# Two weight sums of a seven-product block formed by accumulating DMAs, and three plain blocks per call instead of four

## The chip, the cores and the metric

The kernel runs on one core of one Trainium2 chip. The metric is the device time of one execution in microseconds. Three runs of the kernel before the change took 2412.43, 2413.51 and 2416.30 us; the median is 2413.51 us.

## The reference

The program is two layers of an encoder trunk on 512 tokens of 1024 channels. Each layer has a feed-forward part, a mixer, a cross attention to 256 memory tokens, and a second feed-forward part, so the feed-forward part is called four times. The change touches nothing but this part:

```
def rms_norm(x, g):
    xf = x.astype(jnp.float32)
    y = xf * lax.rsqrt(jnp.mean(xf * xf, axis=-1, keepdims=True) + RMS_EPS)
    return (y * g.astype(jnp.float32)).astype(x.dtype)

def swiglu(x, w_in, w_out):
    gate, up = jnp.split(x @ w_in, 2, axis=-1)
    return (jax.nn.silu(gate) * up) @ w_out

# per layer
x = x + 0.5 * swiglu(rms_norm(x, norm_ffn1[l]), ffn1_wi[l], ffn1_wo[l])
...
x = x + 0.5 * swiglu(rms_norm(x, norm_ffn2[l]), ffn2_wi[l], ffn2_wo[l])
```

The hidden width is 2816, which is 22 blocks of 128.

## The kernel before

Everything is kept with channels on the 128 partitions and the 512 tokens along the free side. A float32 matmul is replaced by three matmuls of float32r operands: every operand is split into a high part, made by a copy on ScalarE (`act`, line 76), and a low part, the rest, made by VectorE (`tt`, line 70, or `stt`, line 73). TensorE then adds high x high, high x low and low x high (`mm3`, line 156; all of its matmuls carry line 79). Weights are split on the chip too, right after they are loaded.

A feed-forward call goes through its 22 hidden blocks f = 0 to 21 in order. For a **plain** block it loads the gate and the up weights of the block (512 KB each, into the tag "raw" with two buffers), splits them, and forms both projections with 2 x 24 matmuls of 512 columns (names `pg`, `pu`). Then it applies the norm's factor, SiLU and the product, and splits the result into `fhi` and `flo`.

For a **seven-product** block ("seven") it takes the gate and up rows of the block as a 2 x 2 matrix of quarters: gate and up, each over the first and the second half of the 1024 input channels. The tokens are halved too, 256 and 256. A Strassen-Winograd scheme then needs seven products of 256 columns instead of eight, that is 7 x 4 x 3 = 84 matmuls of 256 columns. It needs four sums of weight quarters (names `ws` in the profile; s1 to s4 in the code), split parts of seven weight operands (`shi`, `slo`, seven buffers each), and sums of the normed input over channel and token halves (`thi`, `tlo`). The input sums are made once per call by `token_sums`, half of them after plain block 1 and half after plain block 2. Products 1, 2 and 3 use the normed input itself (`hhi`, `hlo`), and products 6, 7, 5 and 4 use the sums (`thi`, `tlo`). The products are issued in the order 1, 2, 6, 3, 7, 5, 4, and VectorE joins their results in `z`, `v` and `u`.

The output projection (`second`, names `wr` for its weights and `po` for its products) is done in parts: the hidden blocks are grouped as 0 to 3, 4 to 9, 10 to 15 and 16 to 21 (`PARTS`), and the output products of one group are mixed into the sevens of the next group, a step at a time (`WO_RATE`). While blocks 0 to 3 run, no output products are pending.

What sets the order: the program is written in the order above, and a scheduler turns it into one in-order list for each engine. Instructions of different blocks get interleaved in these lists. Intermediate tiles of this part (`z`, `u`, `v`, the weight sums, the temporaries of the token sums and of the output products) share the tag "t" with eight buffers. Loads are issued by SP's queue, in order; each waits there until the buffer it writes is free. POOL only adds squares at the end of a call.

Of the kernel before, what the change touches and what calls it, by code (L numbers as in the profile page):

```python
# [8 lines left out]
F32 = mybir.dt.float32  # L9
F32R = mybir.dt.float32r  # L10
AF = mybir.ActivationFunctionType
# [4 lines left out]
T = 512  # L16
# [14 lines left out]
REL_MAX = 256  # L31
LEAD, DENSE_RATE, ATT_RATE = 15, (1.0, 0.61, 0.98), 0.65
TURN_RATE = (0.5, 0.9)
PARTS, PLAIN, WO_RATE, WO_LEAD = (0, 4, 10, 16, 22), 4, 0.85, 2

PAR = {}
_n = 0
# [17 lines left out]
def trunk(tc, I, out, depth=DEPTH):  # L55
    nc = tc.nc
    ctx = ExitStack()
    with ctx:
# [8 lines left out]
        mult, add, sub = ALU.mult, ALU.add, ALU.subtract  # L67

        def tt(o, a, b, op, eng=None):
            (eng or nc.vector).tensor_tensor(out=o, in0=a, in1=b, op=op)  # L70

        def stt(o, a, s, b, op0, op1):
            nc.vector.scalar_tensor_tensor(out=o, in0=a, scalar=s, in1=b, op0=op0, op1=op1)

        def act(o, i, f, **k):
            nc.scalar.activation(out=o, in_=i, func=f, **k)  # L76
# [4 lines left out]
        def t2(name, shape=None, dt=F32):  # L81
            return tp.tile(shape or [P, T], dt, tag="t", name=name, bufs=8)
# [7 lines left out]
        def bank(tag, name):  # L90
            return psp.tile([P, T], F32, tag=tag, name=name, bufs=1 if tag in ("po", "ch") else 2)
# [22 lines left out]
        def load_raw(ap, n, step=1024):  # L114
            raw = wp.tile([P, 1024], F32, tag="raw", name="raw", bufs=2)
            for c in range(0, n, step):
                nc.sync.dma_start(out=raw[:, c:min(c + step, n)], in_=ap[:, c:min(c + step, n)])
            return raw
# [9 lines left out]
        def pc(l, n, j=0):  # L128
            o, w = PAR[n]
            return par[:, l, o + j:o + j + 1]  # L130
# [10 lines left out]
        def split(o_hi, o_lo, src):  # L141
            act(o_hi, src, AF.Copy)
            tt(o_lo, src, o_hi.bitcast(F32), sub)
# [12 lines left out]
        def mm3(p, w, v, first, last):  # L156
            (wh, wl), (vh, vl) = w, v
            mm(p, wh, vh, first, False)
            mm(p, wh, vl, False, False)
            mm(p, wl, vh, False, last)  # L160
# [104 lines left out]
        Q = T // 2  # L265

        def ffn(l, which):
            h = norm(l, f"norm_{which}")
            wi, wo = I[f"{which}_wi"][l], I[f"{which}_wo"][l]
            with tc.tile_pool(name="hid", bufs=1) as hidp:  # L270
# [3 lines left out]
                def out(z, u):  # L274

                    hi = hidp.tile([P, T], F32R, tag="fhi", name="fhi", bufs=11)
                    lo = hidp.tile([P, T], F32R, tag="flo", name="flo", bufs=11)
                    split(hi, lo, u)
                    hid.append((hi, lo))
# [22 lines left out]
                def token_sums(ks):  # L302
                    for k in ks:
                        ga, gb = pc(l, f"norm_{which}", k), pc(l, f"norm_{which}", k + 4)
                        xa, xb = x[k], x[k + 4]
                        b1 = t2("b1")
                        act(b1, xa, AF.Copy, scale=ga)
                        s1, s2 = t2("s12"), t2("s34")
                        stt(s1[:, :Q], xa[:, Q:], ga, b1[:, :Q], mult, sub)
                        stt(s1[:, Q:], xb[:, Q:], gb, s1[:, :Q], mult, sub)  # L310
                        stt(s2[:, :Q], xb[:, Q:], gb, b1[:, Q:], mult, sub)
                        stt(s2[:, Q:], xb[:, :Q], gb, s1[:, Q:], mult, sub)
                        for s in (s1, s2):
                            hi = hidp.tile([P, T], F32R, name=f"thi{len(sums)}")
                            lo = hidp.tile([P, T], F32R, name=f"tlo{len(sums)}")
                            split(hi, lo, s)
                            sums.append((hi, lo))
                    if 3 in ks:
                        hidp.tile([P, 72], F32, name="gap")

                def quarter(n):

                    at = {1: (0, 0), 2: (4, 0), 3: (4, 1)}
                    if n in at:
                        k0, c = at[n]
                        t = h[k0:k0 + 4]
                    else:
                        i, c = {5: (0, 0), 6: (0, 1), 7: (1, 0), 4: (1, 1)}[n]
                        t = sums[i::2]
                    return [(hi[:, c * Q:c * Q + Q], lo[:, c * Q:c * Q + Q]) for hi, lo in t]  # L330

                def seven(f):

                    ra, rb = [load_raw(wi[2 * f + i].rearrange("p k m -> p (k m)"), 1024) for i in range(2)]
                    a11, a12, a21, a22 = ra[:, :T], ra[:, T:], rb[:, :T], rb[:, T:]

                    def parts(src):
                        hi = hidp.tile([P, T], F32R, tag="shi", name="shi", bufs=7)
                        lo = hidp.tile([P, T], F32R, tag="slo", name="slo", bufs=7)
                        split(hi, lo, src)  # L340
                        return hi, lo

                    def sums_of(a, b, op):
                        s = t2("ws")
                        tt(s, a, b, op)
                        return s

                    def product(n, p, c, w):

                        for k, v in enumerate(quarter(n)):  # L350
                            s = slice(k * P, k * P + P)
                            mm3(p[:, c * Q:c * Q + Q], (w[0][:, s], w[1][:, s]), v, not c and k == 0, (c or n == 1) and k == 3)

                    def twice(t, c):
                        return t[:, c * Q:c * Q + Q].unsqueeze(1).to_broadcast([P, 2, Q])

                    two = lambda t: t.rearrange("p (c t) -> p c t", c=2)

                    w1 = parts(a11)
                    w2 = parts(a12)  # L360
                    s1 = sums_of(a21, a22, add)
                    s2 = sums_of(s1, a11, sub)
                    w6 = parts(s2)
                    s4 = sums_of(a12, s2, sub)
                    w3 = parts(s4)
                    s3 = sums_of(a11, a21, sub)
                    w7 = parts(s3)
                    w5 = parts(s1)
                    w4 = parts(a22)
                    pa = bank("acc", "p1")  # L370
                    product(1, pa, 0, w1)
                    p1 = t2("p1")
                    act(p1[:, :Q], pa[:, :Q], AF.Copy)
                    yield
                    pb = bank("iv", "p26")
                    product(2, pb, 0, w2)
                    yield
                    product(6, pb, 1, w6)
                    z = t2("z")
                    tt(two(z), two(pb), twice(p1, 0), add)  # L380
                    yield
                    pb = bank("acc", "p37")
                    product(3, pb, 0, w3)
                    yield
                    product(7, pb, 1, w7)
                    v = t2("v")
                    tt(two(v), two(pb), twice(z, 1), add)
                    yield
                    pb = bank("sm", "p54")
                    product(5, pb, 0, w5)  # L390
                    yield
                    product(4, pb, 1, w4)
                    tt(z[:, Q:], pb[:, :Q], v[:, :Q], add)
                    tt(z, z, r, mult)
                    act(z, z, AF.Silu)
                    u = t2("u")

                    tt(two(u)[:, ::-1], two(pb), twice(v, 1), add)
                    tt(u, u, z, mult)
                    out(z, u)  # L400
                    yield

# [26 lines left out]
                for f0, f1 in zip(PARTS, PARTS[1:]):  # L429
                    for f in range(f0, f1):  # L430
                        if f < PLAIN:
                            plain(f)
                            token_sums({1: (0, 1), 2: (2, 3)}.get(f, ()))
                            continue
                        for _ in seven(f):
                            credit += WO_RATE
                            while credit >= 1:
                                credit -= 1
                                next(wos, None)
                    for _ in wos:  # L440
                        pass
                    wos, credit = second(f0, f1, f1 == KF, ("po", "ch") if f1 < KF else ROT[4:] + ROT[:4]), -WO_LEAD
# [785 lines left out]
```

## Time and profile before

| | |
|---|---|
| median of three runs | 2413.51 us |
| profiled execution | 2414.83 us, span 2413.0 us |
| TensorE (PE) busy | 2370.8 us, 98% of the span |
| VectorE (DVE) busy | 1871.7 us, 78% |
| ScalarE (ACT) busy | 1147.8 us, 48% |
| GpSimd (POOL) busy | 177.2 us, 7% |
| bytes moved by DMA | 225.80 MB, mean 94 GB/s |

Busy times come from one execution on the chip. Instructions on VectorE and ScalarE overlap a little at their ends, so the distance from one start to the next is shorter than the duration shown: a two-input VectorE operation of 128 x 512 elements lasts 0.68 us and the next starts 0.60 us later. The ends of matmuls are modelled. In the chain of waits the profile goes back from the last instruction to what released it, step by step; time that stands there is time that set the end. "Issue to landing" is the time from a DMA's issue until its data is there.

### The profile page before, as it was taken

The numbers are of one execution on the slowest core, as the hardware profiler recorded it, in microseconds if no ns is written. First come the engines' busy times: TensorE is split into PE (matmuls) and PEld (weight loads), VectorE is DVE, ScalarE is ACT, GpSimd is POOL, SyncE is SP. The second block draws the span as 40 slices with busy tenths as digits, with TensorE's granted clock in tenths as the row PEclk, the third lists the DMA queues.
The fourth block names the chain that finished last, engine by engine and source line by source line (L and its number), as shares of the span: only waits on it lengthen the run. The fifth ranks groups of instructions, "written<-read, shape, count | busy, mean of one in ns | idle before, by whom it ended". The sixth has DMA issues, their size and how long they took to land.

```text
span 2413.0 us, 43484 instructions
## 1 busy us (share of the span) xinstructions
PE 2370.8 (98%) x17154; PEld 2046.6 (85%) x17154; DVE 1871.7 (78%) x3423; ACT 1147.8 (48%) x2210; POOL 177.2 (7%) x230
## 2 busy tenths in 40 slices
PE   8999999999999999999999999999999999999999
PEld 6999987787789889999889999767877898899997
DVE  7898876767675669988779988757676756699986
ACT  6444444444565554444454444444445655544443
POOL 1000012011110000000100000120111100000001
PEclk9999999999999999999999999999999999999999
DMA  4323332210342222333332333321103422223332
GB/s 155 106 90 107 103 101 100 70 50 26 92 136 93 94 96 92 112 95 101 96 103 94 97 103 105 110 75 62 50 26 92 138 91 94 97 92 112 96 105 83
DMA packets 90973, 225.80 MB, mean 94 GB/s; under 512 B 10224, under 2 KB 27536, under 8 KB 90768
## 3 DMA queue, kind: packets, MB, share of 16 engines
q1 hardware_dynamic: 90768, 223.01, 28.9%
q8 instruction: 135, 2.21, 0.4%
q14 instruction: 70, 0.57, 0.1%
HBM read 215.89 MB, written 7.08 MB: 92 GB/s over the span
## 4 chain that ended last, share of the span: by engine, by line
PE 90%; DVE 5%; issue 2%; ACT 2%; DMA 1%; POOL 0%; POOLq 0%; ACTq 0%; DVEq 0%; SPq 0%
PE p L79 30%; PE po L79 19%; PE pxq L79 5%; PE pin L79 5%; PE pu L79 3%; PE pxw L79 3%; PE pqk L79 3%; PE pg L79 3%; PE pout L79 3%; PE pbvf L79 1%; PE pf L79 1%; PE ptt L79 1%; DVE wlo L70 1%; PE psc L79 1%; PE pxv L79 1%
## 5 line engine op out<-in xcount | busy, mean ns | idle before, releaser
L70 DVE TENSOR_TENSOR wlo<-raw,whi 128x512 fp32r<-128x512 f32 (+3 forms) x326 | 229.7, 712 | 126.9 <-ACT whi L76 119.3
L79 PE MATMUL p<-thi,shi 128*128 128x256 f32 x1152 | 324.9, 282 | 1.5 <-ACT shi L76 1.4
L79 PE MATMUL p<-tlo,shi 128*128 128x256 f32 x1152 | 323.1, 281 | 0.0
L79 PE MATMUL p<-thi,slo 128*128 128x256 f32 x1152 | 322.9, 282 | 0.0
L76 ACT ACTIVATE whi<-raw 128x512 fp32r<-128x512 f32 (+3 forms) x326 | 194.8, 604 | 249.6 <-PE pin L79 47.0
L79 PE MATMUL po<-flo,whi 128*128 128x512 f32 x704 | 277.4, 394 | 0.0
L79 PE MATMUL po<-fhi,wlo 128*128 128x512 f32 x704 | 277.0, 393 | 0.1
L79 PE MATMUL po<-fhi,whi 128*128 128x512 f32 x704 | 276.5, 394 | 0.0
L79 PE MATMUL p<-hlo,shi 128*128 128x256 f32 x864 | 242.9, 281 | 0.0
L79 PE MATMUL p<-hhi,slo 128*128 128x256 f32 x864 | 242.8, 281 | 0.0
L79 PE MATMUL p<-hhi,shi 128*128 128x256 f32 x864 | 242.7, 281 | 0.0
L79 PEld LDWEIGHTS p<-thi,shi 128*128 128x128 f32 x1152 | 216.8, 188 | 17.9 <-ACT shi L76 10.1
L76 ACT ACTIVATE shi<-ws 128x512 fp32r<-128x512 f32 x288 | 173.8, 629 | 104.1 <-DVE ws L70 102.2
L79 PEld LDWEIGHTS p<-tlo,shi 128*128 128x128 f32 x1152 | 217.0, 188 | 7.2
L79 PEld LDWEIGHTS p<-thi,slo 128*128 128x128 f32 x1152 | 216.1, 188 | 4.0 <-DVE slo L70 1.5
L70 POOL TENSOR_TENSOR ssa<-ssa,sq 128x512 f32<-128x512 f32 x63 | 86.3, 1370 | 1725.7 <-PE po L79 965.1
L76 ACT ACTIVATE whi<-wr 128x512 fp32r<-128x512 f32 x224 | 119.9, 535 | 173.2 <-PE po L79 127.8
L70 DVE TENSOR_TENSOR slo<-ws,shi 128x512 fp32r<-128x512 f32 x288 | 189.2, 683 | 0.0
L70 DVE TENSOR_TENSOR wlo<-wr,whi 128x512 fp32r<-128x512 f32 x224 | 141.2, 637 | 52.5 <-ACT whi L76 51.9
L76 ACT ACTIVATE z<-z 128x512 f32<-128x512 f32 x88 | 55.6, 631 | 257.5 <-DVE z L70 257.4
L76 ACT ACTIVATE shi<-raw 128x512 fp32r<-128x512 f32 x216 | 128.1, 623 | 90.0 <-DMA raw<-in_ffn_wi_dram 89.9
L79 PEld LDWEIGHTS p<-hhi,shi 128*128 128x128 f32 x864 | 162.7, 188 | 4.4 <-ACT shi L76 1.0
(341 smaller groups left out, 5827.2 us busy)
## 6 DMA issues: line engine op xcount, KB each, us to landing
raw<-in_ffn_wi_dram SPq DMA_DIRECT2D x175, 512.0 KB, 3.4
wr<-in_ffn_wo_dram SPq DMA_DIRECT2D x128, 256.0 KB, 3.2
raw<-in_w_in_dram SPq DMA_DIRECT2D x30, 512.0 KB, 3.4
wr<-in_ffn_wo_dram SPq DMA_DIRECT2D x96, 128.0 KB, 2.1
raw<-in_x_wk_dram SPq DMA_DIRECT2D x16, 512.0 KB, 3.8
raw<-in_x_wv_dram SPq DMA_DIRECT2D x16, 512.0 KB, 3.8
raw<-in_x_wq_dram SPq DMA_DIRECT2D x16, 512.0 KB, 3.8
raw<-in_w_qk_dram SPq DMA_DIRECT2D x12, 512.0 KB, 3.8
```

Source lines behind the costliest of these rows:

```text
L70: (eng or nc.vector).tensor_tensor(out=o, in0=a, in1=b, op=op)
L76: nc.scalar.activation(out=o, in_=i, func=f, **k)
L79: nc.tensor.matmul(o, lhsT=w, rhs=x, start=start, stop=stop)
```

## The change

`PLAIN` goes from 4 to 3: block f = 3 of each call becomes a seven, so there are 19 sevens per call instead of 18. The sums `token_sums` makes keep their places (after blocks 1 and 2) but use other signs.

In a seven, s1 and s3 are no longer formed by VectorE. For each of them a new function `loaded` takes a tile of tag "t", has SP load one weight quarter (256 KB) into it, and has GpSimd's queue issue a DMA that adds a second quarter to it. [...] The quarter a21 is then used nowhere alone, so the second load brings only a22 (256 KB).

```
-PARTS, PLAIN, WO_RATE, WO_LEAD = (0, 4, 10, 16, 22), 4, 0.85, 2
+PARTS, PLAIN, WO_RATE, WO_LEAD = (0, 4, 10, 16, 22), 3, 0.85, 2
...
-                        stt(s1[:, :Q], xa[:, Q:], ga, b1[:, :Q], mult, sub)
-                        stt(s1[:, Q:], xb[:, Q:], gb, s1[:, :Q], mult, sub)
+                        stt(s1[:, :Q], xa[:, :Q], ga, b1[:, Q:], mult, sub)
+                        stt(s1[:, Q:], xb[:, Q:], gb, s1[:, :Q], mult, add)
...
-                    ra, rb = [load_raw(wi[2 * f + i].rearrange("p k m -> p (k m)"), 1024) for i in range(2)]
-                    a11, a12, a21, a22 = ra[:, :T], ra[:, T:], rb[:, :T], rb[:, T:]
-
-                    def parts(src):
+
+                    ra = load_raw(wi[2 * f].rearrange("p k m -> p (k m)"), 1024)
+                    a22 = load_raw(wi[2 * f + 1][:, 4:].rearrange("p k m -> p (k m)"), T)[:, :T]
+                    a11, a12 = ra[:, :T], ra[:, T:]
+
+                    def parts(src, sign=None):
                         hi = hidp.tile([P, T], F32R, tag="shi", name="shi", bufs=7)
                         lo = hidp.tile([P, T], F32R, tag="slo", name="slo", bufs=7)
-                        split(hi, lo, src)
+                        if sign:
+                            act(hi, src, AF.Copy, scale=sign)
+                            stt(lo, src, sign, hi.bitcast(F32), mult, sub)
+                        else:
+                            split(hi, lo, src)
                         return hi, lo
+
+                    def loaded(i, j):
+
+                        s = t2("wl")
+                        for (b, k), more in ((i, {}), (j, dict(accum_op=add))):
+                            (nc.gpsimd if more else nc.sync).dma_start(
+                                out=s, in_=wi[2 * f + b][:, 4 * k:4 * k + 4].rearrange("p k m -> p (k m)"), **more)
+                        return s
...
                     w1 = parts(a11)
                     w2 = parts(a12)
-                    s1 = sums_of(a21, a22, add)
-                    s2 = sums_of(s1, a11, sub)
+                    s1, s3 = loaded((1, 0), (1, 1)), loaded((0, 0), (1, 0))
+                    s2 = t2("ws")
+                    stt(s2, s1, -1.0, a11, mult, sub)
                     w6 = parts(s2)
                     s4 = sums_of(a12, s2, sub)
                     w3 = parts(s4)
-                    s3 = sums_of(a11, a21, sub)
                     w7 = parts(s3)
                     w5 = parts(s1)
-                    w4 = parts(a22)
+                    w4 = parts(a22, -1.0)
...
-                    tt(u, u, z, mult)
+                    stt(u, u, -1.0, z, mult, mult)
```

## The prediction

> **What bounds the kernel now.** I read the page's busy shares and its chain of work that ended last, then the busy time in four stretches that hold nearly all blocks of seven products, one per call of the feed-forward part.
>
> ```profile
> PE 2370.8 (98%) x17154; PEld 2046.6 (85%) x17154; DVE 1871.7 (78%) x3423; ACT 1147.8 (48%) x2210; POOL 177.2 (7%) x230
> PE 90%; DVE 5%; issue 2%; ACT 2%; DMA 1%; POOL 0%; POOLq 0%; ACTq 0%; DVEq 0%; SPq 0%
> ```
>
> ```profile
> 64.00:326.00 262.00, 260.62 (x1830) 241.76 (x1829) 236.72 (x400) 116.07 (x215) 0.00 (x0) 1.00 0.32 101
> 905.00:1165.00 260.00, 259.89 (x1826) 241.52 (x1826) 234.04 (x397) 114.10 (x212) 0.00 (x0) 1.00 0.32 100
> 1258.00:1517.00 259.00, 258.93 (x1821) 240.60 (x1821) 233.56 (x395) 113.85 (x211) 0.00 (x0) 1.00 0.32 101
> 2111.00:2371.00 260.00, 259.99 (x1829) 241.71 (x1829) 234.66 (x397) 114.64 (x213) 0.00 (x0) 1.00 0.31 98
> ```
>
> The columns are length, PE, PEld, DVE, ACT, POOL, granted clock, DMA share and GB/s. VectorE is at 90% (234 of 260 us), but PE is idle for only 1.38 + 0.11 + 0.07 + 0.01 = 1.6 us in all four. So VectorE time taken away there buys next to nothing as long as PE stays full; only fewer PE microseconds count, and any new hole in PE is lost. Where PE goes from plain blocks to sevens, the chain of waits of the second call reads:
>
> ```profile
> 883.58 5.44 PE pu L79 x24
> 889.02 5.44 PE pg L79 x24
> 894.46 5.45 PE pu L79 x24
> 899.91 2.84 PE p L79 x24
> 902.74 1.40 PE po L79 x6
> ...
> 1028.31 4.25 PE p L79 x36
> ```
>
> 889.02 to 899.91 is the fourth plain block (f = 3), 10.89 us in two projections. From 899.91 products 1 and 2 of the first seven run. The columns are start, length, what, and how many matmuls; the last row is from later in the same call.
>
> **PE, the certain gain.** A plain block is 48 matmuls of 512 columns, 10.89 us. A seven is 7 x 4 x 3 = 84 of 256 columns at 4.25/36 = 0.118 us, 9.92 us. One block per call changes its kind: -0.97 us, -3.9 us over four calls.
>
> **VectorE and ScalarE per seven.** Two of four weight sums leave VectorE; the other edits swap one two-input operation for another of nearly the same price (`ws<-ws,raw`, `slo<-raw,shi` and `u<-u,z` become scalar_tensor_tensor with a constant, as `po<-po,rstd` is):
>
> ```profile
> L76 ACT ACTIVATE shi<-ws 128x512 fp32r<-128x512 f32 x288 | 173.8, 629 | 104.1 <-DVE ws L70 102.2 <-ACT shi L76 0.2
> L70 DVE TENSOR_TENSOR ws<-raw 128x512 f32<-128x512 f32 x144 | 98.4, 683 | 1.6 <-DMA raw<-in_ffn_wi_dram 1.5
> L73 DVE SCALAR_TENSOR_TENSOR po<-po,rstd 128x512 f32<-128x512 f32 x128 | 87.1, 681 | 7.8 <-PE po L79 7.8
> ```
>
> The first row is ScalarE's high part of a sum. The other two price the change: 144 sums, 98.4 us of VectorE, off an engine that PE covers: 0 us on the path. Without that cover each would count with 0.60 us, since such operations start 0.60 apart (1030.10, 1030.69, 1031.29 in rows below). The token sums keep number and shape, so they cost what they did. The scaled copy on ScalarE is the same instruction with another constant: 0.
>
> **DMA.** Per seven, 2 loads of 512 KB become one of 512, one of 256, two plain of 256 and two accumulating of 256 KB: 768 KB more, or 18 x 0.79 = 14 MB on the 26 MB (262 us x 101 GB/s) of a stretch. The DMA share of 0.32 would go to about 0.5: bandwidth costs 0. SP issues two more per block, behind which the next wr load waits some tenths of a us; PE's hold on its work is longer than that, so 0. POOL is idle in these stretches (0.00), so its two issues push nothing back. Latency is what costs: an accumulating transfer cannot start before the plain one into the same tile has landed, so s1 takes two landings in a row, and s2, then w6, stand behind it.
>
> ```profile
> raw<-in_ffn_wi_dram SPq DMA_DIRECT2D x175, 512.0 KB, 3.4
> wr<-in_ffn_wo_dram SPq DMA_DIRECT2D x128, 256.0 KB, 3.2
> wr<-in_ffn_wo_dram SPq DMA_DIRECT2D x96, 128.0 KB, 2.1
> ```
>
> The plain 256 KB: 3.2 us. The accumulating one, issued from POOL, has no row. From below 2.1 (the shortest landing here), from above 6.4 (it reads its destination as well as its source, so twice 3.2); I take the middle, 4.2, which is the 3.2 of the same size plus a third.
>
> The Trainium skill (DMA: Bandwidth & Descriptors, Anatomy of one DMA — SWDGE (gpsimd) path) gives a DMA issued from GpSimd about 2.0 us plus bytes over 436 GB/s: an estimate of 2.6 us for 256 KB. By it the sum below would come out 1.6 us per call smaller, some 2435 us; no run here shows such a transfer yet.
>
> **The first seven of a call, where the stall goes.** With three plain blocks the seven of f = 3 starts where block f = 3's projection started, at 889.02 in the second call. What VectorE did from there:
>
> ```profile
> 889.05 0.69 DVE L70 TENSOR_TENSOR u<-pu,z 128x512 f32<-128x512 f32 x1 [0.94 <-PE pu L79]
> ...
> 890.26 0.48 DVE L73 SCALAR_TENSOR_TENSOR s<-xs,par,b 128x256 f32<-128x256 f32 x1
> ...
> 895.47 0.48 DVE L73 SCALAR_TENSOR_TENSOR s<-xs,par,s 128x256 f32<-128x256 f32 x1
> 895.86 0.68 DVE L70 TENSOR_TENSOR tlo<-s,thi 128x512 fp32r<-128x512 f32 x1
> ...
> 897.07 0.68 DVE L70 TENSOR_TENSOR tlo<-s,thi 128x512 fp32r<-128x512 f32 x1
> ```
>
> The second half of the token sums (8 `s` at 0.40, 4 `tlo` at 0.60) begins only after u of block f = 2 at 889.05, though VectorE idled 0.94 us just before. I read this as the tiles of the shared tag "t" being handed out in the program's order. These token sums ran under the fourth plain block; that cover goes. PE then has products 1 and 2 of the seven, 2.84 us to 891.86, and nothing else: no output product of an earlier part is pending in f = 0..3, product 6 needs all token sums and w6, product 3 needs s4 and so s2, product 7 needs s3, product 5 s1, and product 4 goes into product 5's bank behind it.
>
> By VectorE alone, product 6 can start after u 0.60, flo 0.60, eight `s` 3.2, four `tlo` 2.4, s2 0.60 = 7.4 us, and the high part of w6 on ScalarE, 0.63 (the row `shi<-ws` has 629 ns): 889.05 + 8.0 = 897.1, a hole of 5.2 us. By the DMA, s1's tile is of tag "t" too and comes behind the token sums' tiles: its load is issued between 889.7 (first slot free after u) and about 892.7 (after u and six `s`); I take 891.2, + 3.2 + 4.2 = 898.6, + s2 0.60 + 0.63 = 899.8, a hole of 7.9 us. Ends: with 889.7 and 2.1 VectorE decides, 5.2 us; with 892.7 and 6.4, 903.5, a hole of 11.6 us. In that hole VectorE waits at s2 as well, with w6, s4, w3 and the z of the block queued behind it, and nobody but PE's product 6 waits for these.
>
> Sum per call: 7.9 - 0.97 = 6.9 us, ends 4.2 and 10.6; over four calls 28 us, ends 17 and 42. The profiled execution took 2414.8 us (span 2413.0 and 1.8 around it), 1.3 above the median 2413.5. So 2414.8 + 28 - 1.3 gives about 2441 us, ends 2430 and 2456.
>
> **In the later sevens** I cost the double landing at nothing, by this cover (second call, VectorE and then SP's queue):
>
> ```profile
> 1030.10 0.68 DVE L70 TENSOR_TENSOR u<-p,v 128x512 f32<-128x512 f32 x1
> 1030.69 0.68 DVE L70 TENSOR_TENSOR z<-z,rstd 128x512 f32<-128x512 f32 x1
> 1031.29 0.68 DVE L70 TENSOR_TENSOR ws<-raw 128x512 f32<-128x512 f32 x1
> ...
> 1044.24 0.68 DVE L70 TENSOR_TENSOR u<-p,v 128x512 f32<-128x512 f32 x1
> ```
>
> ```profile
> 1027.24 2.63 SPq L410 DMA_DIRECT2D wr<-in_ffn_wo_dram  x2
> 1036.34 3.33 SPq L117 DMA_DIRECT2D raw<-in_ffn_wi_dram  x2
> 1040.29 0.93 SPq L410 DMA_DIRECT2D wr<-in_ffn_wo_dram  x2
> ```
>
> The next block's first weight sum again follows u of the block before, so the load of s1 will stand in SP's queue near u, behind the last wr load: 0.2 us ahead of u = 1030.10 by the first row (which ends at 1029.87), about 3 us ahead of the next u, 1044.24, by the third (it ends at 1041.22); I take 1.4. Ready for product 6 at u - 1.4 + 3.2 + 4.2 + 1.2 = u + 7.2. PE has until then products 1 and 2 (done 2.4 us after u: 36 matmuls from 1028.31, of which the first 12 are the block's before) and output products: 16 x 8 x 3 = 384 a call over 18 sevens, 21 at 0.23 = 4.9 us, so u + 7.3. It just fits: no cover beyond 0.1 us.
>
> **Rivals.** First, not slower: token sums and s1 run ahead. If slots are handed out by need, VectorE fills the idle time it has under blocks 0 to 2:
>
> ```profile
> 870.22 0.69 DVE L70 TENSOR_TENSOR z<-pg,rstd 128x512 f32<-128x512 f32 x1 [2.63 <-ACT rstd L76]
> ...
> 872.68 0.69 DVE L70 TENSOR_TENSOR u<-pu,z 128x512 f32<-128x512 f32 x1 [1.18 <-ACT z L76]
> ...
> 878.25 0.69 DVE L70 TENSOR_TENSOR u<-pu,z 128x512 f32<-128x512 f32 x1 [1.60 <-PE pu L79]
> ```
>
> With the 0.94 above that is 6.4 us, more than the 5.6 of the second half. It decides once the token sums end before 890.6 and s1 lands by then. Then only the 3.9 us remain: 2409.6, within 0.2% of before (4.8 us, about what a measurement of this kernel can tell from no change); with the 1.6 us of PE idle above and a little more at the starts of sevens won back, 2404 to 2408, faster. Against it: u comes before the sums in every place that I looked at. Second: the accumulating transfer takes the upper bound, and every seven waits. At 6.4 us product 6 is ready at u + 9.4, 2.1 us late, times 72 later sevens = 151 us on the 2441: 2592; at 5 us 0.7 x 72 = 50: 2491. It decides from 4.3 us on, so the same unknown. For it: nothing but the fit of 0.1 us; against: the queue can run further ahead where wr loads are few. Third, the sums' relief brings no more than the forecast but the hole closes partly (2418 to 2430), if token sums overlap half.
>
> **Chances.** Forecast (2430 to 2456) 0.43; every seven late (2460 to 2592) 0.18; partly closed 0.07; run ahead 0.32, of it 0.20 within 0.2% and 0.12 faster. So slower by over 0.2% 0.68, within 0.20, faster 0.12. The range reaches from 2406, which leaves out some 0.07 of the fast case, to 2500, which leaves out about 0.1 of the late case.
>
> **What would show it.** In the changed profile: `ws<-raw` gone, 12 x 76 = 912 matmuls instead of 864 in each `hhi` group and 1216 instead of 1152 in each `thi` group (PE term right); in each call a hole in PE right after 24 `p` matmuls that follow the third plain block, 5 to 12 us, ended by shi or token sums, with VectorE waiting for a DMA into wl there (forecast); token sums starting before u of block 2 and PE idle under 1 us there (first rival); PE holes of 1 to 2 us in every seven, VectorE waiting for wl some 70 times (second). The forecast is wrong if the four stretches above stay as full and the transition has no hole.

## The result and the profile after

The changed kernel took 2629.81 us (median of four runs, 2627.52 to 2638.33) against 2413.73 us for the kernel before beside it: 1.0900 times as long, 95% interval 1.0885 to 1.0915. The forecast was 2441 us with a range to 2500: the sign was right, the size was not.

The page of the changed kernel, first its busy line, then the chain that ended last, then the groups and DMA issues that answer to those of before (groups end with busy us, mean ns of one, and idle time ahead with its releaser; DMA issues with KB each and median us from issue to landing):

```profile
PE 2446.2 (93%) x17298; PEld 2102.4 (80%) x17298; DVE 1827.4 (70%) x3315; ACT 1152.3 (44%) x2226; POOL 310.0 (12%) x382
...
PE 70%; DVE 13%; DMA 9%; ACT 4%; issue 3%; SPq 0%; POOL 0%; POOLq 0%; ACTq 0%; DVEq 0%
...
L79 PE MATMUL p<-thi,shi 128*128 128x256 f32 x1216 | 360.6, 297 | 115.4 <-ACT shi L76 115.1
...
L353 POOL DMA_DIRECT2D wl<-in_ffn_wi_dram x152 | 132.7, 925 | 1272.4 <-DMA wl<-in_ffn_wi_dram 678.5
...
L79 PE MATMUL p<-hhi,shi 128*128 128x256 f32 x912 | 269.0, 295 | 0.9 <-ACT shi L76 0.9
...
raw<-in_ffn_wi_dram SPq DMA_DIRECT2D x99, 512.0 KB, 3.5
wl<-in_ffn_wi_dram SPq DMA_DIRECT2D x152, 256.0 KB, 3.4
wl<-in_ffn_wi_dram POOLq DMA_DIRECT2D x152, 256.0 KB, 4.5
```

PE's share of the chain fell from 90% to 70%, and DMA's rose from 1% to 9%. PE waits 115 us ahead of `p<-thi,shi`, the products of the token sums, for `shi`, the high part of a weight operand. The products of the plain normed input (`p<-hhi,shi`) wait 0.9 us. So it is the operands made of weight sums that come late, and product 6, which uses s2, is the first of them.

All four stretches of sevens show it, in the columns of the table of stretches in the prediction (length, PE, PEld, VectorE, ScalarE, POOL, granted clock, DMA share, GB/s):

```profile
50.00:383.00 333.00, 299.32 (x1977) 273.03 (x1975) 242.06 (x402) 125.72 (x234) 33.25 (x38) 0.95 0.52 132
941.00:1275.00 334.00, 300.80 (x1986) 274.38 (x1985) 242.62 (x403) 125.62 (x234) 33.19 (x38) 0.95 0.52 132
1346.00:1682.00 336.00, 301.38 (x1985) 274.89 (x1984) 242.69 (x403) 125.73 (x234) 33.15 (x38) 0.95 0.51 131
2252.00:2585.00 333.00, 298.93 (x1987) 272.61 (x1987) 243.16 (x405) 125.71 (x234) 33.08 (x38) 0.95 0.51 129
```

PE is idle for 33.7 + 33.2 + 34.6 + 34.1 = 136 us where it was idle for 1.6, and the granted clock is 0.95 where it was 1.00. The DMA share is 0.52. The time that I measure from the start of a call's first gate matmul to its last output product grew by 52.8, 52.7, 54.4 and 51.6 us, 211.5 of the 212.8 us by which the span grew (2413.0 to 2625.8). Sorting the distances from one matmul start to the next in these calls gives about 145 us more in holes, 60 us more in matmuls that follow each other at a lowered clock, and 4 us less matmul work; some 10 us of the 211.5 this sorting does not assign.

**The first seven of a call**, by the chain of waits of the second call (start, length, what):

```profile
941.99 0.68 DVE u L70
...
944.27 1.98 DVE s L73 x5
946.25 1.20 DVE tlo L70 x2
...
947.94 3.95 DMA wl<-in_ffn_wi_dram
951.89 0.02 issue
951.91 0.70 DVE ws L73
...
953.32 9.86 PE p L79 x60
```

SP issues the plain load of s1's tile at 943.67, u + 1.68, while the token sums run behind u of block 2. It lands at 947.40, and the accumulating DMA starts 0.54 us behind it, at u + 5.95, and lands at u + 9.90; then s2, and product 6 at u + 11.3. (The chain puts the token sum `s` ahead of the accumulating DMA, because it ended at 947.87; but in 74 of the 76 sevens the accumulating DMA starts 0.50 to 0.60 us after the plain one has landed, so the landing is the likelier cause.)

**A later seven**, in two kinds. VectorE's order from u on (start, length, line, operation, and in brackets the idle time before it and what ended it), one seven of each kind:

```profile
1014.30 0.68 DVE L70 TENSOR_TENSOR u<-p,v 128x512 f32<-128x512 f32 x1
...
1017.66 0.69 DVE L70 TENSOR_TENSOR flo<-u,fhi 128x512 fp32r<-128x512 f32 x1 [0.70 <-ACT fhi L76]
1019.51 0.69 DVE L70 TENSOR_TENSOR wlo<-wr,whi 128x512 fp32r<-128x512 f32 x1 [1.16 <-ACT whi L76]
1020.12 0.68 DVE L73 SCALAR_TENSOR_TENSOR ws<-wl,raw 128x512 f32<-128x512 f32 x1
...
1029.82 0.68 DVE L70 TENSOR_TENSOR u<-p,v 128x512 f32<-128x512 f32 x1
...
1037.16 0.69 DVE L73 SCALAR_TENSOR_TENSOR ws<-wl,raw 128x512 f32<-128x512 f32 x1 [0.91 <-DMA wl<-in_ffn_wi_dram]
```

SP's queue and GpSimd's issues of the same time:

```profile
1009.29 0.86 SPq L353 DMA_DIRECT2D wl<-in_ffn_wi_dram  x2
...
1028.87 0.33 SPq L424 DMA_DIRECT2D wr<-in_ffn_wo_dram  x1
1029.25 0.90 SPq L353 DMA_DIRECT2D wl<-in_ffn_wi_dram  x2
```

```profile
1012.83 1.75 POOL L353 DMA_DIRECT2D wl<-in_ffn_wi_dram  x2 [15.37 <-DMA wl<-in_ffn_wi_dram]
1032.91 1.75 POOL L353 DMA_DIRECT2D wl<-in_ffn_wi_dram  x2 [18.34 <-DVE u L73]
```

In the second of the two (u at 1029.82) the plain load of s1 is issued only 0.6 us ahead of u, right behind a `wr` load; the accumulating one follows 3.7 us later, and s2 starts at u + 7.3, ended by that DMA. In the first, the loads were issued 5.0 us ahead of u and s1 had landed before 1017; there s2 starts at u + 5.8 because VectorE's list has `flo` and `wlo` ahead of it, and `wlo` waits for ScalarE. By the landing times in the trace, 34 of the 76 sevens are of the kind that waits for the landing (s2 within 0.3 us of it), and 42 of the other. PE's holes right ahead of product 6 add up to 125 us: 21 in the four first sevens of a call, 58 in the 30 later ones that wait for the landing, and 46 in the 42 others. In the kernel before, the first weight sum stood in the list directly behind `z`, 1.2 us after u.

### The profile page after: what moved, and what is told of

Its sections match the earlier page's. It is cut to its first block, busy times and chain, and to the rows that moved or that the text cites. A ratio compares the mean times of both kernels' runs of the same rounds, so it can differ in the third digit from the quotient of the medians.

```text
span 2625.8 us, 44395 instructions
## 1 busy us (share of the span) xinstructions
PE 2446.2 (93%) x17298; PEld 2102.4 (80%) x17298; DVE 1827.4 (70%) x3315; ACT 1152.3 (44%) x2226; POOL 310.0 (12%) x382
## 4 chain that ended last, share of the span: by engine, by line
PE 70%; DVE 13%; DMA 9%; ACT 4%; issue 3%; SPq 0%; POOL 0%; POOLq 0%; ACTq 0%; DVEq 0%
PE p L79 23%; PE po L79 12%; DMA wl<-in_ffn_wi_dram 7%; PE pxq L79 5%; PE pin L79 4%; PE pxw L79 3%; PE pqk L79 3%; DVE wlo L70 3%; PE pout L79 3%; PE pu L79 2%; PE pg L79 1%; PE pbvf L79 1%; ACT whi L76 1%; DVE slo L70 1%; PE pf L79 1%
## 5 line engine op out<-in xcount | busy, mean ns | idle before, releaser
L79 PE MATMUL p<-thi,shi 128*128 128x256 f32 x1216 | 360.6, 297 | 115.4 <-ACT shi L76 115.1
L79 PE MATMUL p<-thi,slo 128*128 128x256 f32 x1216 | 359.9, 296 | 11.5 <-DVE slo L70 11.4
L79 PEld LDWEIGHTS p<-thi,shi 128*128 128x128 f32 x1216 | 241.6, 199 | 143.1 <-ACT shi L76 140.0
L79 PE MATMUL p<-tlo,shi 128*128 128x256 f32 x1216 | 354.2, 291 | 0.0
L353 POOL DMA_DIRECT2D wl<-in_ffn_wi_dram x152 | 132.7, 925 | 1272.4 <-DMA wl<-in_ffn_wi_dram 678.5
L79 PE MATMUL p<-hhi,shi 128*128 128x256 f32 x912 | 269.0, 295 | 0.9 <-ACT shi L76 0.9
L79 PEld LDWEIGHTS p<-thi,slo 128*128 128x128 f32 x1216 | 242.5, 199 | 22.7 <-DVE slo L70 20.6
L79 PEld LDWEIGHTS p<-tlo,shi 128*128 128x128 f32 x1216 | 242.1, 199 | 2.9
L79 PEld LDWEIGHTS p<-hlo,shi 128*128 128x128 f32 x912 | 183.7, 201 | 2.4
L79 PEld LDWEIGHTS p<-hhi,slo 128*128 128x128 f32 x912 | 183.0, 201 | 0.0
```

Of the source, the lines that this page charges most:

```text
L79: nc.tensor.matmul(o, lhsT=w, rhs=x, start=start, stop=stop)
L353: (nc.gpsimd if more else nc.sync).dma_start(out=s, in_=wi[2 * f + b][:, 4 * k:4 * k + 4].rearrange("p k m -> p (k m)"), **more)
```

## The experiments

**Four plain blocks, sums by DMA.** The changed kernel with one number put back:

```
-PARTS, PLAIN, WO_RATE, WO_LEAD = (0, 4, 10, 16, 22), 3, 0.85, 2
+PARTS, PLAIN, WO_RATE, WO_LEAD = (0, 4, 10, 16, 22), 4, 0.85, 2
```

> The changed kernel with four plain blocks again: the sums by accumulating DMAs alone. Theory A (two landings in a row stand in front of product 6 of every seven): the first seven of a call gets its cover back, and its block time of 21.6 to 22.3 us in the changed kernel goes back to the 10.9 us of a plain block, 4 x 10.7 = 43 us less than 2630: 2587 (2575 to 2600); the 72 later sevens keep their loss of about 2.3 us each. Theory B (the extra traffic and POOL's transfers slow the whole part, wherever they stand): 72 of 76 sevens keep it, 2618.

Measured: 2595.05 us (2592.30 to 2603.00), 1.0756 times before (1.0730 to 1.0783). So the sums by DMA alone cost about 180 us, and taking away the fourth plain block costs the 35 us between this and the changed kernel. From the first product to the last, the sevens of a call take 309 to 320 us, where they took 269 to 271 in the kernel before.

**Three plain blocks, sums on VectorE.** The kernel before with the same number changed the other way:

```
-PARTS, PLAIN, WO_RATE, WO_LEAD = (0, 4, 10, 16, 22), 4, 0.85, 2
+PARTS, PLAIN, WO_RATE, WO_LEAD = (0, 4, 10, 16, 22), 3, 0.85, 2
```

> The kernel before with three plain blocks: the count alone, all four sums on VectorE. Theory A, by the prediction's path over VectorE: a hole of 5.2 us in front of product 6 of the first seven, less 0.97 us of matmuls, 4.2 x 4 = 17 us: 2431 (2425 to 2440). Theory B: no extra traffic, so only the matmuls count: 2410.

Measured: 2434.34 us (2432.76 to 2436.73), 1.0083 times before (1.0068 to 1.0098), some 20 us. The second call's first seven, as PE ran it (start, length, and in brackets the idle time and its end); u of block 2 is at 895.57:

```profile
897.82 0.40 PE L79 MATMUL po<-fhi,whi 128*128 128x512 f32 x1
...
901.72 0.39 PE L79 MATMUL po<-fhi,wlo 128*128 128x512 f32 x1
904.35 0.39 PE L79 MATMUL p<-thi,shi 128*128 128x256 f32 x1 [2.24 <-ACT shi L76]
...
905.50 0.58 PE L79 MATMUL p<-thi,slo 128*128 128x256 f32 x1 [0.64 <-DVE slo L70]
```

Product 6 starts at u + 8.8; VectorE is busy through all of it with token sums and weight sums, so this part of the loss needs no DMA. Two things were not foreseen: 18 output products fill 4.1 us of the gap (more on them below), and a call is 5 us longer all the same. By the distances between matmul starts, the four calls have 16 us more in holes than before (in this call also one of 0.95 us ahead of product 6 of the next seven), some 8 us in matmuls that run slower after holes, and 4 us less matmul work.

**One landing.** The first experiment without the accumulating DMAs. In the changed kernel the up half of the weights enters negated, so that both sums are plain additions, s1 = a21 + a22 and s3 = a11 + a21; here each is one weight quarter in place of the sum of two:

```
-for (b, k), more in ((i, {}), (j, dict(accum_op=add))):
+for (b, k), more in ((i, {}),):
```

> As e1_plain4, with the accumulating DMAs left out, so that s1 and s3 are one weight quarter each instead of a sum of two: one landing in front of s2 instead of two, half of the added bytes. Theory A: a landing of 4.5 us goes, more than the 2.3 us that a later seven loses, so nearly all is back: 2414 to 2440. Theory B: half of the added traffic stays, about half of the loss: 2500.

Measured: 2427.29 us (2425.84 to 2429.82), 1.0054 times before (1.0039 to 1.0070). 168 of the 180 us are gone with the second landing. This alone does not say whether its latency or its traffic, POOL's issues included, did it.

**Loads a block ahead, in another tag.** The first experiment with the tiles of s1 and s3 taken from tag "b" (`b2`, six buffers, which in this part hold only the `wr` loads) in place of "t", and issued one seven earlier in the program (`fetch(f)` issues the loads of block f):

```
-s = t2("wl")
+s = b2("wl")
...
-s1, s3 = loaded((1, 0), (1, 1)), loaded((0, 0), (1, 0))
+s1, s3 = early.pop(f) if f in early else fetch(f)
+if f + 1 < KF:
+    early[f + 1] = fetch(f + 1)
```

> As e1_plain4, with the same loads and accumulating DMAs, but their tiles come from the buffers of wr (tag b) and they are issued one seven ahead, so that both landings lie under the products of the seven before. Theory A: no seven waits for s1 any more, PE is full as before the change: 2405 to 2425. Theory B: the same bytes by the same queues cost the same: 2587 to 2618, as e1_plain4.

Measured: 2439.41 us (2436.51 to 2442.04), 1.0103 times before (1.0086 to 1.0120). The bytes and the number of issues are those of the first experiment and the loss is nearly gone, so the traffic is not the cause. But it is 14 us above what I expected at most. Its sevens take 272 to 274 us a call, which makes 12 of the 22 us by which its span (2434.7 us) is longer than before. From the first gate matmul to the last output product its four calls are 15 us longer together, so the other 7 us lie outside the part that the edit touches. What the early issue costs in both places I did not find; whether sharing six buffers with the `wr` loads has a part in it was not tried.

**The tag alone.** The same without the early issue, so that one line differs from the first experiment:

```
-s = t2("wl")
+s = b2("wl")
```

> As e1_plain4 (2595 us), but the tiles of s1 and s3 come from tag b, where they stand behind the wr tiles and not behind u of the seven before; nothing is issued a seven ahead in the program. Theory A1 (the order of tag t is what makes s1 late): its loads can go some us earlier and the planner sees it, so at least half of the 180 us comes back: 2430 to 2510. Theory A2 (what is lacking is issue a whole seven ahead): 2560 to 2595.

Measured: 2424.32 us (2419.62 to 2428.64), 1.0041 times before (1.0028 to 1.0053). I had expected that the program's order would still hold the loads back; it does not. The tag by itself returns 171 us. (It is the tag of the `wr` loads; an expectation further down calls it a tag of their own, which it is not.) One stretch of this run, and s2's place in VectorE's list in one of its sevens:

```profile
905.00:1165.00 260.00, 258.39 (x1817) 240.91 (x1816) 213.55 (x361) 109.89 (x210) 26.87 (x31) 1.00 0.59 151
```

```profile
960.15 0.68 DVE L70 TENSOR_TENSOR u<-p,v 128x512 f32<-128x512 f32 x1
...
961.95 0.68 DVE L73 SCALAR_TENSOR_TENSOR ws<-wl,raw 128x512 f32<-128x512 f32 x1
```

More traffic than in the changed kernel (share 0.59, 151 GB/s) and a full PE. The load of s1 is now issued 22 us or more ahead of u (26 in the median), s2 starts within 2 us of u, and in all 72 sevens s1 has landed at least 14 us before s2. VectorE has 20.5 us less to do in this stretch than in the same one of the kernel before (213.55 against 234.04), as the change was to give, and the time is 10 us above before: there was hardly any PE time to win. This edit changes when the loads run and with it VectorE's list, so it does not part the two kinds of late sevens from each other.

**Three landings.** The first experiment with the second quarter added twice (so s1 and s3 hold one quarter too many):

```
-for (b, k), more in ((i, {}), (j, dict(accum_op=add))):
+for (b, k), more in ((i, {}), (j, dict(accum_op=add)), (j, dict(accum_op=add))):
```

> As e1_plain4, with the second quarter added twice, so s1 and s3 are not the sums the scheme needs: three landings in a row in front of s2 instead of two. Theory A: 4.2 us more stand in front of product 6 in each of 72 sevens, 302 us on 2595, and some more by the lowered clock: 2880 to 2960. If the second landing had been partly hidden and the loss were order alone, under 100 us: below 2700.

Measured: 2705.48 us (2702.27 to 2708.70), 1.1205 times before (1.1180 to 1.1230). A third landing adds 110 us, 1.5 us for each of 72 sevens, not the 4 that a wait for the landing in every seven would give. This is the miss that showed the two kinds of sevens: with two landings only 32 of these 72 wait for the landing, with three 49 do, and the others have slack that takes the third landing in. The plain load of s1 is also issued earlier, 5.1 us ahead of u in the mean instead of 3.4.

**Token sums earlier.** The kernel before with three plain blocks and the token sums after blocks 0 and 1 in place of 1 and 2:

```
-token_sums({1: (0, 1), 2: (2, 3)}.get(f, ()))
+token_sums({0: (0, 1), 1: (2, 3)}.get(f, ()))
```

> The kernel before with three plain blocks (e2_plain3, 2434 us) and the token sums made after plain blocks 0 and 1 instead of 1 and 2. If the hole of the first seven was the second half of the token sums under no cover, it closes, and only the matmuls saved remain, 0.97 us x 4: 2409 to 2413 against 2413.5 to 2415 of before. If VectorE is short of time for another reason, it stays near 2434.

Measured: 2418.14 us (2416.32 to 2421.36), 1.0017 times before (1.0008 to 1.0026). It returns 16 of the 20 us of the second experiment, and the holes ahead of product 6 of the first sevens are gone (2.4 us in the mean there, 0.03 here), so that hole was the token sums' place. It is 5 us above what I expected and still wins nothing. The chain of waits around the start of the second call's first seven shows why:

```profile
885.23 2.08 PE pg L79 x9
...
889.71 0.69 DVE tlo L70
890.40 1.19 DVE s L73 x3
...
895.04 2.66 PE p L79 x20
```

The sums and u of block 2 now stand ahead of `slo`, the low part of a weight that the seven's first product needs, and PE waits 1.1 us for it (up to 895.04).

**Both at once.** The loads a block ahead, three plain blocks and early token sums: the edits of the fourth experiment and of the one just above together.

> Sums by accumulating DMAs issued one seven ahead (e4_ahead, 2439 us), three plain blocks, token sums after blocks 0 and 1. With the first seven covered it is e4_ahead less 0.97 us x 4: 2435. If what e4_ahead still loses against before came from VectorE's list and not from the transfers, VectorE's spare time shows nothing here either: no faster than before (over 2414).

Measured: 2448.26 us (2446.05 to 2456.37), 1.0146 times before (1.0126 to 1.0165), 13 us above what I expected, as the fourth experiment was.

**The changed kernel with the tag alone**, one line of it:

```
-s = t2("wl")
+s = b2("wl")
```

> The changed kernel with one edit: the tiles of s1 and s3 come from a tag of their own in place of the shared tag t; three plain blocks, everything else as changed. Theory (the loss of the later sevens is the shared tag's order, the hole of the first seven is the token sums' order and does not hang on the tag): the same kernel with four plain blocks took 2424, three plain blocks without the sums by DMA cost 21 over before, so 2424 + 21 = 2445, range 2435 to 2450; first seven of a call 18 to 20 us, down from 22, because s1 is loaded before u of block 2; sevens 270 to 273 us in 18 of a call. Rival (the first seven's hole is the double landing as predicted): first seven stays at 21 to 22 us, 2455 to 2465. Rival (tag matters only with four plain blocks): above 2500.

Measured: 2455.77 us (2451.48 to 2458.06), 1.0162 times before (1.0145 to 1.0179). One stretch of it:

```profile
902.00:1190.00 288.00, 282.62 (x1981) 263.72 (x1981) 236.44 (x402) 123.74 (x234) 28.55 (x33) 0.99 0.55 149
```

PE is idle for 5.4 us where the changed kernel has 33.2, and 174 of its 216 us are back. The first seven of a call takes 17.5 to 18.7 us where the changed kernel has 21.6 to 22.3, about as expected, since its s1 no longer waits behind the token sums. The total is 6 us above the range that I had given. It falls into that of the first rival, but the sign of that rival, a first seven that stays at 21 to 22 us, is absent. The third seven of a call takes 15.1 to 18.0 us here and 13.3 in the second experiment, and why was not tried.

**The same with early token sums**, the edit of the experiment on token sums:

> The same with the token sums after blocks 0 and 1. Theory: the first seven drops to 13 to 15 us and the plain blocks lose some 2 to 3 us per call, as they did without the sums by DMA (2418, 4 over before); with the 10 us that the sums by DMA cost with four plain blocks, 2428, range 2415 to 2435. Not faster than before. If PE had gained from VectorE's relief, under 2409.

Measured: 2436.12 us (2431.30 to 2441.64), 1.0084 times before (1.0065 to 1.0103), 1 us above the range. The first seven falls to 13.5 us in three of four calls. No version of the sums by DMA came out faster than before.

The medians side by side (the kernel before took 2413.7 to 2415.9 us beside these runs):

| | four plain blocks | three |
|---|---|---|
| sums on VectorE | 2414 (before) | 2434 |
| sums by DMA, tag "t" | 2595 | 2630 (the change) |
| sums by DMA, tag "b" | 2424 | 2456 |

## Why the prediction was right and wrong

**What was right.** "PE, the certain gain": `hhi` groups of 912 and `thi` groups of 1216 matmuls are there, so one block per call did change its kind. "Bandwidth costs 0": the share was put at 0.5 and is 0.52, and the experiment with the other tag runs at 0.59 with a full PE. The accumulating DMA was put at 4.2 us; its row has 4.5 from issue to landing, the median of all 152, and those into s1's tile, which alone stand ahead of s2, have 4.2 in the mean. The sum lacked the 0.56 us (median) between the plain landing and the start of the accumulating DMA: from the plain issue to the second landing it has 7.4 us, and the trace 8.0 in the mean. "VectorE time taken away there buys next to nothing": with the tag changed, VectorE has 20 us less per stretch and the time is not shorter.

**The first seven** was near: 6.9 us per call net, 28 in all, against 35 us between the first experiment and the changed kernel. Product 6 was put at 899.8 in the trace of before, u + 10.8, and starts at u + 11.3. The reading that tiles of the tag "t" are handed out in the program's order held too. One sentence of that step failed: "no output product of an earlier part is pending". In the trace, 18 output products of blocks 0 to 2 stand in this gap, 4.1 us, in the second experiment's rows and in the changed kernel alike. The scheduler pulls them forward as soon as these blocks exist; it does not wait until the part of four is complete. In the second call that cuts the idle time to 4.9 us, with work that is only moved there from later.

**The step that failed is the cover in the later sevens**: "384 output products/18 = 21 per seven = 4.9 us, so u + 7.3". It counts all output products of a seven as if they stood ahead of product 6. The chain of waits of the kernel before, right after the row at 1028.31 that I had read, shows where they stand:

```profile
1032.56 1.41 PE po L79 x6
1033.97 0.23 PE p L79 x2
1034.20 0.70 PE po L79 x3
...
1036.09 0.70 PE po L79 x3
...
1038.21 1.39 PE po L79 x6
...
```

Six of them, 1.41 us, are ahead of product 6, which starts here 3.7 us after u = 1030.10 (at 1033.81); the rest are spread over the whole seven. Over the 68 later sevens of the kernel before, PE is filled until u + 4.6 in the mean (3.2 to 6.5), with 9 output products between u and product 6, not 21. My time for product 6, u + 7.2, was close: in the changed kernel it is u + 7.7 in the mean of 72 later sevens. 7.2 - 4.6 = 2.6 us, times the 68 later sevens of the first experiment = 177 us; the sums by DMA cost it 180 us. (That they agree so well is partly luck: see the next paragraphs, and the sum leaves out the holes in that run's four first sevens, 11 us.) So the case that I had called the second rival was the case, at the middle value of the accumulating transfer and not at its upper bound: the point from which it decides, 4.3 us, was worked out from the same false cover. With u + 4.6 it is 4.6 + 1.4 - 3.2 - 1.2 = 1.6 us, below the lower end that I had given the transfer, 2.1: it would have been late in any case. The measured 2630 us lie above even the 2592 that I had put at that rival's upper end.

**Two things inside it were other than I thought.** I put s1's load at u - 1.4; in the mean it is at u - 3.5, and in 42 of 76 sevens s1 is there in time, but VectorE's list has `flo` and `wlo` ahead of s2, so that s2 comes late all the same (u + 5.0 in their mean, and u + 7.6 in that of the 34 that wait for the landing). That a list written for a late operand stays late when the operand is early was in no rival. And the changed kernel's order has more output products ahead of product 6 (16 in the mean, so that PE is filled until u + 6.2), which leaves a hole of 1.4 us per seven, 104 us in 72: less than 2.6 each.

**A term was missing**: matmuls after a hole often run slower (last section). It is worth some 60 of the 213 us, and makes up for most of what the holes are shorter.

**What the runs do not settle**: how the loss splits between the landing and VectorE's list, since the one line that changes the tag changes both, and a list made for a late operand may owe its order to the landing (the holes by kind, 58 and 46 us, are as far as the trace goes); and the 14 us of the loads a block ahead.

## What to carry to other kernels

Before work is called cover, find where it stands: read the chain between the very instruction that starts the wait and the one that ends it, and do not spread a mean over the block. A tile that is loaded ahead needs a tag that lets it be loaded ahead: in the tag shared with late temporaries its load was issued 3.5 us ahead of u in the mean, in that of the `wr` loads 22 us or more (here 171 us for one line). And an engine at 90% beside a full PE has nothing to give back, however much is taken off it.

## What was not expected of the hardware

**Idle time in short holes lowered the clock.** PE in the changed kernel around two holes in one seven (start, length, and in brackets the idle time and what ended it):

```profile
985.95 0.39 PE L79 MATMUL po<-fhi,wlo 128*128 128x512 f32 x1
987.35 0.39 PE L79 MATMUL p<-thi,shi 128*128 128x256 f32 x1 [1.01 <-ACT shi L76]
...
988.76 0.39 PE L79 MATMUL p<-thi,slo 128*128 128x256 f32 x1 [0.91 <-DVE slo L70]
988.98 0.28 PE L79 MATMUL p<-thi,shi 128*128 128x256 f32 x1
989.10 0.29 PE L79 MATMUL p<-tlo,shi 128*128 128x256 f32 x1
...
990.04 0.41 PE L79 MATMUL p<-thi,shi 128*128 128x256 f32 x1
990.26 0.41 PE L79 MATMUL p<-tlo,shi 128*128 128x256 f32 x1
...
992.75 0.28 PE L79 MATMUL p<-hlo,shi 128*128 128x256 f32 x1
992.86 0.28 PE L79 MATMUL p<-hhi,slo 128*128 128x256 f32 x1
```

The matmuls right behind the two holes still follow each other 0.12 us apart (988.98 to 989.10). From 989.40 to 992.60 there are 15 of 256 columns that are 0.21 us apart, then it is 0.12 again. The table of short stretches (columns as above) has the granted clock beside it, for these holes and for a longer one that cost no clock:

```profile
985.82:989.23 3.41, 1.49 (x9) 0.86 (x8) 2.26 (x4) 2.45 (x5) 0.00 (x0) 1.00 0.14 42
989.23:992.64 3.41, 3.41 (x19) 3.41 (x18) 3.41 (x7) 2.18 (x5) 0.00 (x0) 0.50 0.47 165
1122.35:1125.76 3.41, 1.94 (x9) 1.28 (x7) 0.74 (x2) 0.42 (x1) 0.86 (x1) 1.00 0.82 119
1125.76:1129.18 3.42, 2.38 (x17) 2.17 (x18) 3.42 (x7) 3.37 (x7) 0.00 (x0) 1.00 0.76 195
```

In the second pair there is a distance of 2.59 us between two matmuls (1123.90 to 1126.49) and the clock stays at 1.00, so the length of one hole does not decide. What the trace shows instead is a grid: in this run the clock is at 0.50 in 33 stretches, 150 us together, and all of them begin on one grid of steps of 3.41 us, on which the stretches above are cut. PE was idle for 1.92 us in the step ahead of the drop; the longer hole falls into two steps, of which one has 1.47 us of idle and the other 1.04. Of the 36 steps at full clock in which PE was idle for 1.57 us or more, 33 are followed by a step at 0.50, and of the 686 others none is. So in this trace it was idle time of about half a step that lowered the clock for the next one, in one hole or in several. The kernel before has 13.5 us at 0.50, so 137 us were added; half of that, 68 us, is an upper estimate of what the lowered clock cost, as PE had holes in these steps too, and the sorting above has 60.

The Trainium skill (TensorE: Matmul & The Clock Gate, Part 1: The HAM clock gate) has half rate after an idle window of about 3.4 us and full rate again after about 3.4 us of work. The rate here comes near it, 0.12 against 0.21 us, and so does the length of the slow stretch, 3.41 us; that a whole window must be idle does not, as PE was idle for only 1.92 of 3.41 us ahead of it.

**The accumulating DMA** of 256 KB takes 4.5 us from issue to landing, in the table of DMA issues above, beside 3.4 for the plain one into the same kind of tile, and each issue keeps POOL busy for 0.9 us (152 of them, 132.7 us). The Trainium skill (DMA: Bandwidth & Descriptors, Anatomy of one DMA — SWDGE (gpsimd) path) has the fit from which the estimate of 2.6 us in the prediction is worked out; the trace does not agree with it for a transfer that accumulates. No run here has a plain transfer from POOL beside it, so how much of the difference is the adding stays open.
